# First four MLP slabs by seven products, MLP weight sums by accumulating transfers, rotary work offered to GpSimd: a two-layer fp32 encoder on one core

## The chip, the core and the metric

The kernel runs on 1 core of one Trainium2 chip. TensorE (PE) multiplies; VectorE (DVE), ScalarE (ACT) and GpSimd (POOL) work on elements; SyncE (SP) issues the loads and stores. The metric is the device time of one execution in microseconds. Three runs of the kernel before gave 1735.47, 1737.61 and 1735.81 us, a median of 1735.81.

## The reference

Two requests (256 and 512 tokens, each with 16 meta tokens put ahead: 272 + 528 = 800) go through an encoder trunk of two layers, width 1024, with shared weights:

```
for i in range(2):
    mix = mla_mixer(h, ...) if i == 0 else gqa_mixer(h, ...)
    h = layer_norm(ALPHA * h + mix)
    h = layer_norm(ALPHA * h + (relu(h @ w1) ** 2) @ w2)
return h[:, 16:]
```

The mixer of layer 0 is latent attention (dense, 16 heads, a rotary part of 32 rows for each head and one rotary key for all); the mixer of layer 1 is windowed attention with grouped heads. w1 is 1024 x 4096, w2 4096 x 1024. All is fp32 and is compared in fp32 precision.

## The kernel before

**Arithmetic.** A product in fp32 is made of three matmuls (`mm3`, L545, its matmuls L546, L547, L548): each operand is split into a high part (fp32r, a cast on ACT) and a low part (the rest, a subtraction on DVE), and high x high, high x low and low x high are summed in PSUM. Splits of weights are at L1538 (ACT) and L1544 (DVE), of hidden values at L1581 and L1583.

**Seven products for eight.** Where two output slabs and two halves of the tokens form a 2 x 2 block, the kernel uses the Strassen-Winograd scheme: seven products of blocks instead of eight, for some sums of operands before and of results after. In the input projection this is `pair` (L760 to L803), in the MLP `up_pair` for x @ w1 and `down_group` for the second product. Sums of weight blocks are made on chip by `weight_add` (L1549, the instruction L1555): a tensor_tensor on DVE or POOL over 512 columns. Sums of hidden values are `minus` (L1587, the instruction L1589); results are added to the residual by `accumulate` (L1849, L1851).

**The MLP.** It has 32 slabs of 128 hidden rows. The first four (`UP_FIRST`) are made one by one with plain products (`up_slab`), first on the first half of the tokens, while the layer norm of the attention is still being finished, then on the second. `down_first` (L1912) multiplies these four slabs with their rows of w2 in the conventional way: in layer 0 4 tiles x 2 halves x 2 outputs x 4 steps x 3 = 192 matmuls of 400 columns, in layer 1, where tokens stand on the output's partitions, 2 x 6 x 2 x 2 x 3 = 144 matmuls of 512 columns. In layer 1 the residual is turned by PE transposes (L1724) that lie between these matmuls (`TURNS`). Then six groups follow (`GROUPS`), each of two `up_pair`s (four slabs) and a `down_group` over both; the last four slabs end the layer. Weight tiles come by SP loads (L1513) of 512 KB into four raw buffers (`wraw`, with one more, `wx`), go through sums and splits, and stand in four split buffers (`wsp`) and one of half size (`w22`).

**What sets the order.** In the input projection the order on an engine is that of the code. From the attention on, tasks are handed to `Plan`, a list scheduler with costs for each engine; it can give a task to either of two engines where the code offers both (`either`, `other=`), and the order of PE's tasks comes from tables of numbers (`ORDERS`), one for each plan. Each engine runs its queue in order.

**Attention of layer 0.** For each head pair the rotary rows of the queries are made on DVE (multiply by the cosine, shuffle, multiply by the sine L1028, add, split) and copied into the heads' operand tiles (`qcopy`, L1036, 64 casts on 32 partitions). The probabilities are scaled on POOL (L1207). The rotary key's projection (`key_rope`, L604) is eight steps over the input rows, into one PSUM tile `pkr`, each step issued when its part of the input has come.

Of the kernel before, what the change touches and what calls it, by code (L numbers as in the profile page):

```python
# [20 lines left out]
P = 128  # L21
# [62 lines left out]
UPN = len(UP_FIRST)  # L84
LAST = 28
GROUPS = [(j, j + 2) for j in range(UPN, LAST, 4)]

TURNS = {1: (0, 0), 2: (0, 1), 3: (1, 0), 5: (1, 1)}  # L90
DOWN_ORDERS = ((7, 1, 6, 5, 3, 4, 2), (1, 7, 6, 5, 3, 2, 4))
# [55 lines left out]
class Plan:  # L147
# [4 lines left out]
    LAG = {"PE": 198, "DVE": 45, "ACT": 45, "POOL": 50, "SP": 0}  # L152
# [4 lines left out]
    OVER = {"PE": 0, "DVE": 82, "ACT": 100, "POOL": 30, "SP": 0}  # L157
# [56 lines left out]
    def lag(self, i, k):  # L214
        a, b = self.tasks[i][0], self.tasks[k][0]
        if a == "PE" or a == "SP":
            return 0 if a == b or a == "SP" else 198
        return {"PE": 90, "POOL": 78}.get(b, 34)

    def hold(self, i, e, cost):  # L220
        if self.thin[i]:
            return cost + 20
        return cost / 2 if e == "SP" else max(cost - self.OVER[e], cost / 2)

# [238 lines left out]
def tile_encoder(ctx: ExitStack, tc: tile.TileContext, ins: dict, y):  # L463
# [81 lines left out]
    def mm3(out, lh, ll, rh, rl, start, stop, **kw):  # L545
        nc.tensor.matmul(out, lh, rh, start=start, stop=False, **kw)  # L546
        nc.tensor.matmul(out, lh, rl, start=False, stop=False, **kw)  # L547
        nc.tensor.matmul(out, ll, rh, start=False, stop=stop, **kw)  # L548
# [16 lines left out]
    def sq_tile(pool, nm):  # L565
        return pool.tile([P, HALF], F32, tag="sq", name=f"sq{nm}", bufs=6)
# [28 lines left out]
    with ExitStack() as st:  # L595
# [6 lines left out]
        def key_rope(k, xr, c):  # L602
            for i in range(c.start // KR, c.stop // KR):
                nc.tensor.matmul(  # L604
                    pkr[32 * i : 32 * i + 32], wkr[:, k], xr[:, i * KR : (i + 1) * KR],
                    start=k == 0, stop=k == 7, tile_position=(0, 32 * i), skip_group_check=True,
                )

        for k in range(8):
# [5 lines left out]
            for c in [slice(0, HALF), slice(HALF, NT)] if k < 2 else [slice(0, NT)]:  # L615
                nc.sync.dma_start(xr[:, c], ins["xT0"][k][:, c])
                key_rope(k, xr, c)
                split(x[0][:, k, c], x[1][:, k, c], xr[:, c])
            if k % 2 == 0:
                for i in (1, 2):  # L620
                    slices[i][k // 2](nc.sync if k else None)
# [140 lines left out]
        def pair(o, u, w22, steps):  # L762
# [12 lines left out]
            def product(ps, w, c0, ops, start, stop):  # L775
                for k in range(4):
# [697 lines left out]
    def mlp_middle(mp, sqp, late_sum, T, n, l, tiles, yt=None, txs=None, ends=None):  # L1474
# [437 lines left out]
        def down_first():  # L1912
# [25 lines left out]
            for r in range(2):  # L1938
# [3 lines left out]
                for i, t in [(i, t) for t in range(6) for i in range(2)] if r == 0 else [(i, t) for a in (0, 3) for i in range(2) for t in range(a, a + 3)]:  # L1942
                    if r == i == 0 and t in TURNS:
                        turn(*TURNS[t])
                        for f in behind:
                            f()
# [790 lines left out]
```

## Time and profile before

| | |
|---|---|
| time, median of three runs | 1735.81 us |
| the profiled execution | 1735.74 us |
| its span | 1733.9 us |
| input projection | 0 to 82.5 us |
| attention of layer 0 | 82.5 to 452 us |
| MLP of layer 0 | 452 to 923 us |
| attention of layer 1 | 923 to 1234 us |
| MLP of layer 1 (last matmul) | 1234 to 1725 us |
| DVE busy, of its 2999 instructions | 1443.8 us |
| POOL busy | 220.7 us |
| bytes moved by the DMA engines | 122.32 MB |

How to read it: a time is in microseconds from the start of the span unless marked ns. A row of a timeline gives start, duration, engine, line, operation, out<-in and shape, and, in brackets, how long the engine had stood idle and what released it. A group of instructions has a count, busy time and the mean of one, then the idle time just before. A row of waits gives the total, how often and the longest. Matmuls are pipelined, so that one begins before the last has ended: the distance of two starts, and not the duration of a record, is what a matmul costs. Numbers at the end of tile names are left out in the trace; in the order rows below they are kept.

### The profile page before, as it was taken

The numbers are of one execution on the slowest core, as the hardware profiler recorded it, in microseconds if no ns is written. First come the engines' busy times: TensorE is split into PE (matmuls) and PEld (weight loads), VectorE is DVE, ScalarE is ACT, GpSimd is POOL, SyncE is SP. The second block draws the span as 40 slices with busy tenths as digits, with TensorE's granted clock in tenths as the row PEclk, the third lists the DMA queues.
The fourth block names the chain that finished last, engine by engine and source line by source line (L and its number), as shares of the span: only waits on it lengthen the run. The fifth ranks groups of instructions, "written<-read, shape, count | busy, mean of one in ns | idle before, by whom it ended". The sixth has DMA issues, their size and how long they took to land.

```text
span 1733.9 us, 28692 instructions
## 1 busy us (share of the span) xinstructions
PE 1720.2 (99%) x10826; PEld 1616.7 (93%) x10826; DVE 1443.8 (83%) x2999; ACT 1025.7 (59%) x2176; POOL 220.7 (13%) x228
## 2 busy tenths in 40 slices
PE   9999999999999999999999999999999999999998
PEld 8999999999999999999999998889989889988996
DVE  7698888986978889889886978875887899889977
ACT  6577777783745446445644728775665446545652
POOL 1211111112200000000002333232300000011000
PEclk9999999999999999999999999999999999999999
DMA  6111011104311212122123312111311221222122
GB/s 231 59 32 41 11 46 31 35 30 155 109 50 61 74 64 71 64 83 74 53 69 104 101 61 79 41 50 50 122 49 62 73 73 62 74 73 74 64 90 79
DMA packets 39019, 122.32 MB, mean 71 GB/s; under 512 B 4704, under 2 KB 9952, under 8 KB 38752
## 3 DMA queue, kind: packets, MB, share of 16 engines
q1 hardware_dynamic: 38448, 120.09, 20.8%
q8 instruction: 85, 1.39, 0.3%
q14 instruction: 54, 0.44, 0.1%
q10 hardware_dynamic: 432, 0.39, 0.1%
HBM read 117.32 MB, written 3.15 MB: 69 GB/s over the span
## 4 chain that ended last, share of the span: by engine, by line
PE 95%; DVE 3%; ACT 1%; issue 0%; DMA 0%; SPq 0%; DVEq 0%; ACTq 0%
PE w L547 18%; PE w L546 18%; PE w L548 18%; PE wb L546 4%; PE wb L547 4%; PE wb L548 4%; PE wa L546 3%; PE wa L547 3%; PE wa L548 3%; PE wa L1271 2%; PE wa L1238 2%; PE sa L546 2%; PE wb L2439 2%; PE sa L547 2%; PE sa L548 2%; PE wb L2421 2%
## 5 line engine op out<-in xcount | busy, mean ns | idle before, releaser
L1851 DVE TENSOR_TENSOR acc<-acc,w 128x400 f32<-128x400 f32 (+1 forms) x306 | 185.2, 620 | 35.2 <-PE w L548 33.4
L546 PE MATMUL w<-h,wsp 128*128 128x400 f32 x324 | 111.8, 345 | 0.0
L547 PE MATMUL w<-h,wsp 128*128 128x400 f32 x324 | 111.7, 345 | 0.0
L548 PE MATMUL w<-h,wsp 128*128 128x400 f32 x324 | 111.4, 344 | 0.0
L547 PE MATMUL w<-h,wspi 128*128 128x400 f32 x308 | 106.2, 345 | 0.0
L548 PE MATMUL w<-h,wspi 128*128 128x400 f32 x308 | 106.0, 344 | 0.0
L546 PE MATMUL w<-h,wspi 128*128 128x400 f32 x308 | 105.9, 344 | 0.0
L1583 DVE TENSOR_TENSOR h<-sq,h 128x384 fp32r<-128x384 f32 (+1 forms) x164 | 93.4, 579 | 8.8 <-ACT h L1581 8.0
L1581 ACT CAST h<-sq 128x384 fp32r<-128x384 f32 (+1 forms) x164 | 83.7, 519 | 21.7 <-DVE sq L1589 12.5
L1180 ACT ACTIVATE p<-sa,nm,rq 106x528 f32<-106x528 f32 (+1 forms) x80 | 63.5, 794 | 26.4 <-DVE nm L1177 21.4
L1207 POOL TENSOR_TENSOR p<-p,rs 106x512 f32<-106x512 f32 (+1 forms) x40 | 43.7, 1094 | 252.3 <-DVE pk L1198 139.3
L546 PE MATMUL w<-wsp,h 128*128 128x512 f32 (+1 forms) x176 | 69.3, 394 | 0.0
L548 PE MATMUL w<-wspi,h 128*128 128x512 f32 (+1 forms) x176 | 69.1, 393 | 0.0
L546 PE MATMUL w<-wspi,h 128*128 128x512 f32 (+1 forms) x176 | 69.1, 393 | 0.0
L547 PE MATMUL w<-wspi,h 128*128 128x512 f32 (+1 forms) x176 | 69.1, 393 | 0.0
L548 PE MATMUL w<-wsp,h 128*128 128x512 f32 (+1 forms) x176 | 69.1, 393 | 0.0
L547 PE MATMUL w<-wsp,h 128*128 128x512 f32 (+1 forms) x176 | 69.1, 393 | 0.0
L546 PE MATMUL sa<-k,q 128*106 128x264 f32 (+5 forms) x208 | 63.2, 304 | 1.1 <-ACT p L1190 0.7
L1762 ACT COPY sq<-w 128x400 f32<-128x400 f32 (+1 forms) x70 | 34.0, 486 | 48.5 <-PE w L548 47.9
L546 PEld LDWEIGHTS w<-h,wsp 128*128 128x128 f32 x324 | 60.9, 188 | 0.4 <-ACT sq L1762 0.2
L547 PEld LDWEIGHTS w<-h,wsp 128*128 128x128 f32 x324 | 60.8, 188 | 0.2
L548 PEld LDWEIGHTS w<-h,wsp 128*128 128x128 f32 x324 | 60.9, 188 | 0.0
(827 smaller groups left out, 6048.4 us busy)
## 6 DMA issues: line engine op xcount, KB each, us to landing
wrawo<-in_w_o_dram SPq DMA_DIRECT2D x32, 512.0 KB, 3.3
wraw0d<-in_w2b_dram SPq DMA_DIRECT2D x24, 512.0 KB, 3.3
wraw1d<-in_w2b_dram SPq DMA_DIRECT2D x18, 512.0 KB, 3.2
wrawq<-in_w_q_dram SPq DMA_DIRECT2D x8, 512.0 KB, 3.3
xr<-in_xT_dram SPq DMA_DIRECT2D x16, 200.0 KB, 3.3
wraw<-in_w_qn_dram SPq DMA_DIRECT2D x8, 384.0 KB, 3.1
wx1d<-in_w2b_dram SPq DMA_DIRECT2D x6, 512.0 KB, 4.2
out_dram<-fo SPq DMA_DIRECT2D x11, 256.0 KB, 2.0
```

What stands on the lines that cost most here:

```text
L546: nc.tensor.matmul(out, lh, rh, start=start, stop=False, **kw)
L547: nc.tensor.matmul(out, lh, rl, start=False, stop=False, **kw)
L548: nc.tensor.matmul(out, ll, rh, start=False, stop=stop, **kw)
L1180: lambda: S.activation(P_().rearrange("p (a b) -> p a b", b=264), v(), AF.Exp, bias=nm.t[:qm, 0:1], scale=sc, accum_out=rs.t[:qm, 0:1]),
L1207: f = lambda row=row, r=r, w=w: G.tensor_tensor(row()[:, META:T], row()[:, META:T], r().to_broadcast([qm, w]), ALU.mult)
L1238: nc.tensor.transpose(ps.t[:, k * qm : (k + 1) * qm], src[k], ident[:qm, :qm])
L1271: nc.tensor.matmul(av[64 * e : 64 * e + 64, :n], vt.t[:, k, h0 + 64 * e : h0 + 64 * e + 64], PT.t[:, e, k, :n], start=k == 0, stop=False, ...
L1581: plan.task("ACT", 530, lambda: S.copy(d.t[:, 0], c.t[:, :n]), reads=[c], writes=[(d, "hi")], new=[d])
L1583: "DVE", 570, lambda: V.tensor_tensor(d.t[:, 1], c.t[:, :n], d.t.bitcast(F32)[:, 0], ALU.subtract),
L1851: f = lambda: V.tensor_tensor(z, z, ps.t[:, : z.shape[-1]], ALU.add)
L2421: nc.tensor.transpose(ps.t[:, n * P : (n + 1) * P], SM.t[:, a : a + P], ident)
L2439: nc.tensor.matmul(av[64 * gi : 64 * gi + 64, :256], at["V"][:, kbs[k][0], gc : gc + 64], PT.t[:, a : a + 256], start=k == 0, stop=False, ...
```

## The change

1. `down_first` is gone. The first four slabs keep their results on the first half of the tokens (`kept`; the pool of such tiles has 8 buffers for 6), and their operands for the seven products are made like those of any group. `down_group(0, first, None)` multiplies them; w2's rows for them come as a group more (`FIRST_PAIRS`), and layer 1's transposes are all issued ahead of it.
2. Sums of weight blocks are made by transfers: `sum_in` issues, on POOL's queue, a transfer from the weights in HBM that adds to what stands in the raw tile. Each of the 28 up pairs has 4 of these of 256 KB, each of the 14 groups' down products 4 of 512 KB: 168. The blocks that a sum needs are read from HBM again. A transfer can only add, so signs are rearranged: the splits of some operands take the negative (a factor of -1 on ACT, a scalar_tensor_tensor on DVE), a relu gets the scale -1, and half of the results are subtracted.
3. In the attention of layer 0, some rotary work may go to POOL: the multiplication by the sine, the sum, the low parts of y and of the attention's result, the copies of `qcopy` and the low copies of the rotary key. 57 of the 64 casts of `qcopy` do.
4. In the input projection, the steps k = 2 to 7 of the rotary key are issued in pairs, and in `pair` the second half of the last Z product (6 matmuls) is put after the X product.
5. Two of the products' orders and the four PE tables are new.

```diff
+        def sum_in(out, src):
+            r, c = out
+            key = parts(r, c)
+            plan.task("SUM", 4500, lambda: nc.gpsimd.dma_start(r.t[:, c], src, accum_op=ALU.add), reads=key, writes=key)
...
             w22 = new("w22", lambda: mp.tile([P, 2, 512], F32R, tag="w22", name=f"w22{l}_{j}", bufs=1))
+            sum_in((b, lo), w1[j + 1][:, hi])
             split_weights(ua, lo, a, lo)
-            weight_add((a, lo), (a, lo), (b, lo), ALU.subtract, 512)
-            weight_add((b, lo), (b, lo), (b, hi), ALU.add, 512)
             split_weights(ua, hi, b, lo)
-            weight_add((b, lo), (b, hi), (a, lo), ALU.subtract, 512)
+            sum_in((b, lo), w1[j][:, lo])
+            sum_in((a, lo), w1[j + 1][:, lo])
             split_weights(ub, lo, b, lo)
-            weight_add((b, lo), (a, hi), (b, lo), ALU.subtract, 512)
+            sum_in((b, lo), w1[j][:, hi])
             split_weights(ub, hi, b, lo)
...
             out = {x: weights(f"{l}d{g}_{x}") for x in DOWN_ORDERS[l]}
-            weight_add((A21, c), (A11, c), (A21, c), ALU.subtract, w)
...
+            sum_in((A21, c), src[2, :, :w])
+            split_weights(out[1], c, A11, c)
+            sum_in((A11, c), src[1, :, :w])
+            split_weights(out[7], c, A11, c)
+            split_weights(out[5], c, A21, c)
+            sum_in((A21, c), src[0, :, :w])
+            A22 = get(2)
             split_weights(out[6], c, A21, c)
+            sum_in((A21, c), src[3, :, :w])
...
-            F[j, 0] = split_hidden(up_slab(j, 0, ws[j], twos, fill.get(j)))
+            up_slab(j, 0, ws[j], twos, fill.get(j), kept[j])
+            if j in (1, 2):
+                operands_be(first[j // 2], kept[j & 2], kept[j | 1])
...
-            F[j, 1] = split_hidden(up_slab(j, 1, w, [range(k, k + 1) for k in range(8)] if j == 0 else [range(8)]))
-        down_first()
-        for g, js in enumerate(GROUPS):
+            d = up_slab(j, 1, w, [range(k, k + 1) for k in range(8)] if j == 0 else [range(8)])
+            if j % 2 == 0:
+                operands_a(first[j // 2], kept[j], kept[j + 1], d)
+            else:
+                operands_r(first[j // 2], kept[j - 1], d)
+        if turn:
+            for hf, q in TURNS:
+                turn(hf, q)
+        down_group(0, first, None)
+        for g, js in enumerate(GROUPS, 1):
             down_group(g, [{} for _ in js], js)
...
-            plan.task("DVE", DVE(n), lambda: V.tensor_tensor(sh.t[:, :n], sh.t[:, :n], sinq[:, a:b], ALU.mult), reads=[sh], writes=[sh], port=True)
+            plan.task("DVE", DVE(n), lambda: turned(V), reads=[sh], writes=[sh], port=True, other=("POOL", POOL(n), lambda: turned(G)))
...
-            product(X, u[2], 0, TS[2], False, False)
+            x_ends = product(X, u[2], 0, TS[2], False, False)
...
-            product(Z, u[2], 512, B[1][1::2], True, True)
+            z_ends = product(Z, u[2], 512, B[1][1::2], True, True)
+            after(z_ends[2][0], x_ends[3][1])
...
-DOWN_ORDERS = ((7, 1, 6, 5, 3, 4, 2), (1, 7, 6, 5, 3, 2, 4))
+DOWN_ORDERS = ((1, 7, 6, 5, 3, 4, 2), (1, 7, 6, 5, 3, 2, 4))
...
-    "0 2-6 11 1 12 7-8 10 13-14 9 20 15 17 16 18-19 21 23 22 24 26-30 32-33 31 35 34 37 36 39 38 40 25 41-43 45 44 47-48 46 50 49 51-52"
+    "0 3 2 4-5 8 6 9 7 1 12-13 11 10 16 14 17 15 20 19 18 23 21-22 29 24 26-28 30 32 31 25 33 35 37-40 36 34 41 46 42 45 44 47-49 51 "
```

Where it moves instructions. On PE, in the input projection's `pair`, before (`inx`, `iny`, `inz` are the banks X, Y, Z; `w22i` is the last product's weight):

```order
361 L548 MATMUL iny_740<-x_134,wspi_687 128x400
362 L548 MATMUL inz_741<-x_134,wspi_724 128x400
363 L546 MATMUL inx_739<-some,wspi_724 128x400
...
373 L547 MATMUL inx_739<-tk_249,wspi_724 128x400
374 L548 MATMUL inx_739<-w22i,wspi_724 128x400
375 L546 MATMUL inx_739<-x_134,w22i 128x400
```

and after:

```order
367 L550 MATMUL inx_739<-tk_249,wspi_724 128x400
368 L551 MATMUL inx_739<-w22i,wspi_724 128x400
369 L549 MATMUL inz_741<-x_134,wspi_724 128x400
370 L550 MATMUL inz_741<-x_135,wspi_724 128x400
371 L551 MATMUL inz_741<-x_134,wspi_724 128x400
372 L549 MATMUL inz_741<-x_134,wspi_724 128x400
373 L550 MATMUL inz_741<-x_135,wspi_724 128x400
374 L551 MATMUL inz_741<-x_134,wspi_724 128x400
375 L549 MATMUL inx_739<-x_134,w22i 128x400
```

Before, the Z product was over when X's began, and X's last product follows X directly; now six matmuls of Z stand between.

On POOL, at the start of the MLP of layer 0, before (`tsum` and `sq` are sums of activations, `wraw` raw weight tiles):

```order
88 L1683 TENSOR_TENSOR tsum_5635<-acc 128x400
89 L1683 TENSOR_TENSOR tsum_5635<-acc,tsum_5635 128x400 x2
90 L1589 TENSOR_TENSOR sq_4_5697<-sq_4_5697,sq_3_5682 128x400
91 L1555 TENSOR_TENSOR wraw0d_6773<-wraw0d_6952,wraw0d_6773 128x512
92 L1589 TENSOR_TENSOR sqsum_5193<-sqsum_5193,sq_1_5671 128x400
```

and after:

```order
168 L1577 DMA wraw0d_5708<-in_w2b_dram 128x1024
169 L1708 TENSOR_TENSOR tsum_5635<-acc 128x400
170 L1577 DMA wraw0d_5684<-in_w2b_dram 128x1024
171 L1577 DMA wraw0d_5708<-in_w2b_dram 128x1024 x2
172 L1614 TENSOR_TENSOR sq_5_5700<-sq_3_5682,sq_5_5700 128x400
173 L1614 TENSOR_TENSOR sq_2_5673<-sq_3_5682,sq_2_5673 128x400
174 L1577 DMA wraw_4b<-in_w_0_dram 128x512
175 L1614 TENSOR_TENSOR sq_0_5657<-sq_4_5697,sq_0_5657 128x400
176 L1577 DMA wraw_4a<-in_w_0_dram 128x512
177 L1577 DMA wraw_4b<-in_w_0_dram 128x512
```

POOL's queue now holds the transfers of the weight sums in line with its sums of activations.

On PE, the rotary key's steps after (before, each stood alone between other matmuls):

```order
44 L550 MATMUL in_487<-x_135,wsp_65 128x400
45 L608 MATMUL pkr<-xr_180,wkr 32x200 x4
46 L608 MATMUL pkr<-xr_167,wkr 32x200 x4
47 L550 MATMUL in_255<-x_135,wsp_61 128x400
```

Two steps follow each other, and of the six visits for k = 2 to 7 three are left.

More of the change, by code (lines that the diff above doesn't have):

```diff
@@ L147 @@
 class Plan:
-    LAG = {"PE": 198, "DVE": 45, "ACT": 45, "POOL": 50, "SP": 0}
+    LAG = {"PE": 198, "DVE": 45, "ACT": 45, "POOL": 50, "SP": 0, "SUM": 0}
     CHANGE = {
@@ L156 @@
     }
-    OVER = {"PE": 0, "DVE": 82, "ACT": 100, "POOL": 30, "SP": 0}
+    OVER = {"PE": 0, "DVE": 82, "ACT": 100, "POOL": 30, "SP": 0, "SUM": 0}
     last, count = {}, 0
@@ L215, in lag @@
         a, b = self.tasks[i][0], self.tasks[k][0]
-        if a == "PE" or a == "SP":
-            return 0 if a == b or a == "SP" else 198
-        return {"PE": 90, "POOL": 78}.get(b, 34)
+        if a in ("PE", "SP", "SUM"):
+            return 198 if a == "PE" != b else 0
+        return {"PE": 90, "POOL": 78, "SUM": 78}.get(b, 34)
     def hold(self, i, e, cost):
@@ L222, in hold @@
             return cost + 20
-        return cost / 2 if e == "SP" else max(cost - self.OVER[e], cost / 2)
+        return cost / 2 if e == "SP" else 1300 if e == "SUM" else max(cost - self.OVER[e], cost / 2)
     def forward(self, deps, after, late):
@@ L545, in mm3 @@
     def mm3(out, lh, ll, rh, rl, start, stop, **kw):
-        nc.tensor.matmul(out, lh, rh, start=start, stop=False, **kw)
+        first = nc.tensor.matmul(out, lh, rh, start=start, stop=False, **kw)
         nc.tensor.matmul(out, lh, rl, start=False, stop=False, **kw)
-        nc.tensor.matmul(out, ll, rh, start=False, stop=stop, **kw)
+        last = nc.tensor.matmul(out, ll, rh, start=False, stop=stop, **kw)
+        return first.ins, last.ins
     def after(a, b):
@@ L854, in new, with split_to @@
             return plan.held(tag, make)
-        def split_to(out, view, name, reads, n, ends=(), thin=False):
+        def split_to(out, view, name, reads, n, ends=(), thin=False, pool=False):
             plan.task("ACT", ACT(n), lambda: S.copy(out()[0], view()), reads=reads, writes=[(name, "hi")], ends=ends, thin=thin)
+            rest = lambda on: on.tensor_tensor(out()[1], view(), out()[0].bitcast(F32), ALU.subtract)
             plan.task(
-                "DVE", DVE(n), lambda: V.tensor_tensor(out()[1], view(), out()[0].bitcast(F32), ALU.subtract),
-                reads=[*reads, (name, "hi")], writes=[(name, "lo")], port=True, ends=ends, thin=thin,
+                "DVE", DVE(n), lambda: rest(V), reads=[*reads, (name, "hi")], writes=[(name, "lo")], port=True, ends=ends, thin=thin,
+                other=("POOL", POOL(n), lambda: rest(G)) if pool else None,
             )
@@ L1034, in qcopy @@
                 for i, x in enumerate(("hi", "lo")):
+                    f = lambda on, e=e, i=i, row=row: on.tensor_copy(Q[s][e][i][ROPE[e] : ROPE[e] + 32], YW[s][i].bitcast(F32)[row : row + 32])
                     plan.task(
-                        "DVE", 165 + 0.5 * n, lambda e=e, i=i, row=row: V.tensor_copy(Q[s][e][i][ROPE[e] : ROPE[e] + 32], YW[s][i].bitcast(F32)[row : row + 32]),
-                        reads=[(("y", s, a), x) for a, _ in SEQ[s][3]], writes=[(("qr", s, e), x)], thin=True,
+                        "DVE", 165 + 0.5 * n, lambda f=f: f(V), reads=[(("y", s, a), x) for a, _ in SEQ[s][3]], writes=[(("qr", s, e), x)],
+                        thin=True, other=("POOL", 200 + 0.8 * n, lambda f=f: f(G)),
                     )
@@ L1067, in krope @@
                             to = K[s][e][x][r, a - 272 * s : b - 272 * s]
[L1068 removed]
+                            plan.task(
+                                on, cost(b - a), lambda copy=copy, view=view, to=to: copy(to, view), writes=[(("kr", s, e, i), ("hi", "lo")[x])],
+                                port=x == 1, ends=[st1], thin=True,
+                                other=("POOL", 200 + 0.8 * (b - a), lambda view=view, to=to: G.tensor_copy(to, view)) if x else None,
+                            )
         V_ = {}
@@ L1761, in copy @@
             def copy(d, ps, f=AF.Copy):
-                plan.task("ACT", 500, (lambda: S.copy(d.t[:, :n], ps.t[:, :n])) if f is AF.Copy else (lambda: S.activation(d.t[:, :n], ps.t[:, :n], f)), reads=[ps], writes=[d], new=[d])
+                plan.task(
+                    "ACT", 500, (lambda: S.copy(d.t[:, :n], ps.t[:, :n])) if f is AF.Copy else (lambda: S.activation(d.t[:, :n], ps.t[:, :n], f, scale=-1.0)),
+                    reads=[ps], writes=[d], new=[d],
+                )
             def plus(d, ps):
@@ L1883, in part @@
                     if ps[-1] == len(ops) - 1:
-                        accumulate(place(r, q, hf)[0], banks[q], place(r, q, hf)[1])
+                        accumulate(place(r, q, hf)[0], banks[q], place(r, q, hf)[1], ALU.subtract if r else ALU.add)
             def product(*args):
@@ L1969, in mlp_middle @@
         fill = {UP_FIRST[0]: {0: mean}, UP_FIRST[1]: {3: sums}, UP_FIRST[2]: {1: scale}}
-        F = {}
+        first = [{}, {}]
+        kept = {j: tmp(f"k{l}_{j}") for j in range(4)}
         for j in UP_FIRST:
```

186 lines of the change are left out of this document (75 added, 111 removed), and 77 rows, old and new, of the table ORDERS.

## The prediction

> **What bounds the kernel now.** I read the page first: the engines' shares and the chain that ended last.
>
> ```profile
> span 1733.9 us, 28692 instructions
> PE 1720.2 (99%) x10826; PEld 1616.7 (93%) x10826; DVE 1443.8 (83%) x2999; ACT 1025.7 (59%) x2176; POOL 220.7 (13%) x228
> PE 95%; DVE 3%; ACT 1%; issue 0%; DMA 0%; SPq 0%; DVEq 0%; ACTq 0%
> ```
>
> TensorE is busy for 99% of the span and makes up 95% of the chain. The profiled run took 1735.74 us: 1.84 us lie outside its 1733.9 us span. The three timed runs are 1735.47, 1735.81 and 1737.61, so the profiled run is the median but for 0.07 us, and what I take off its time I take off the median. Next come the stages, with columns of stretch, length, then PE, PE weight load, DVE, ACT, POOL, granted clock, DMA share, GB/s: attention of layer 0, half of its MLP, and half of the MLP of layer 1.
>
> ```profile
> 90.00:452.00 362.00, 359.78 (x2984) 335.92 (x2984) 310.37 (x859) 258.06 (x644) 62.83 (x53) 1.00 0.17 54
> 452.00:690.00 238.00, 237.82 (x1310) 236.97 (x1309) 202.51 (x341) 132.69 (x241) 12.77 (x11) 1.00 0.19 63
> 1234.00:1480.00 246.00, 245.11 (x1258) 220.94 (x1258) 213.64 (x343) 138.23 (x259) 12.86 (x11) 1.00 0.21 69
> ```
>
> The clock is full in all of them, and the MLP stretches leave PE idle for 0.18 of 238 and 0.89 of 246 us. DVE is the second engine (202.5 of 238 there, 85%). So time goes where matmuls go, or where one of PE's few idle places closes. Busy shares hide how dense PE is, since matmuls overlap: starts show that. In the timeline of PE, 128x400 and 128x512 matmuls:
>
> ```profile
> 499.79 0.35 PE L547 MATMUL w<-h,wspi 128*128 128x400 f32 x1
> ...
> 501.99 0.34 PE L547 MATMUL w<-h,wsp 128*128 128x400 f32 x1
> 1290.54 0.40 PE L547 MATMUL w<-wsp,h 128*128 128x512 f32 x1
> ...
> 1291.93 0.39 PE L547 MATMUL w<-wsp,h 128*128 128x512 f32 x1
> ```
>
> From 499.79 to 501.99 are 12 steps: 0.183 us each. From 1290.54 to 1291.93 are 6: 0.232 us each. These are the prices of one matmul, not the 0.35 and 0.39 that each record lasts.
>
> **The change, part by part.**
>
> *Down projection of the first four slabs.* By the conventional method it takes 192 matmuls of 400 columns in layer 0 and 144 of 512 in layer 1; by seven products of eight it takes 168 and 126. The order of the new program has 42 PE rows fewer, as this says. 24 x 0.183 + 18 x 0.232 = 4.39 + 4.18 = **8.57 us off**, straight from the bounding engine. Its new operands cost nothing on the path: each layer needs 14 splits of hidden operands where it had 8, and eight sums.
>
> ```profile
> L1583 DVE TENSOR_TENSOR h<-sq,h 128x384 fp32r<-128x384 f32 (+1 forms) x164 | 93.4, 579 | 8.8 <-ACT h L1581 8.0
> L1589 DVE TENSOR_TENSOR sq<-sq,sq 128x400 f32<-128x400 f32 (+1 forms) x52 | 31.3, 604 | 0.2
> L1555 DVE TENSOR_TENSOR wraw0d<-wraw0d,wraw0d 128x512 f32<-128x512 f32 x46 | 30.9, 686 | 1.5 <-DMA wraw0d<-in_w2b_dram 1.5
> ```
>
> 6 x 0.579 + 8 x 0.604 = 8.3 us of DVE, beside the second half of the four slabs, 4 x 24 x 0.183 = 17.6 us of PE. It fits if DVE has nothing else; at 85% busy it doesn't quite. What is late then is the first group's operands, and the cover is that the group begins with products 1 and 7, whose operands are made first. In layer 1 all transposes of the residual now stand ahead of the group, where before they lay between matmuls. I cost both at nothing, bounded by 0 and 2 x 8.3 / 2 = 8 us (half of that DVE work bare, in both layers). In return DVE loses the weight sums, 30.9 us in the row above alone.
>
> *Weight sums by transfers.* 168 accumulating transfers, issued on POOL's queue, take over from DVE. No trace of before shows one. The chain that grows is that of an up pair. Here is the first pair of a group in layer 0: the cast that waited for its raw tile, the last split of the third sum, and the matmul that uses it:
>
> ```profile
> 571.74 0.62 ACT L1538 CAST w<-wraw_8b 128x512 fp32r<-128x512 f32 x1 [1.01 <-DMA wraw_8b<-in_w_dram]
> 585.97 0.69 DVE L1544 TENSOR_TENSOR wspi<-wraw_8b,wspi 128x512 fp32r<-128x512 f32 x1 [0.69 <-ACT wspi L1538]
> 593.75 0.34 PE L546 MATMUL w<-h,wspi 128*128 128x400 f32 x1
> ACT wspi L1538 <- PE w L547: 44.3, 28, 4.5
> ```
>
> The weight is ready at 586.66 and used at 593.75: 7.1 us early; and ACT's splits wait for buffers that PE frees (44.3 us in 28 waits), so the weights run ahead. In the new order three sums and three splits follow one another: 3s + 3 x (0.62 + 0.69) must fit into 593.75 - 571.74 = 22.0 us, so s may be **6.0 us**. The nearest rows for s, from the list of transfers:
>
> ```profile
> wraw0d<-in_w2b_dram SPq DMA_DIRECT2D x24, 512.0 KB, 3.3
> wx1d<-in_w2b_dram SPq DMA_DIRECT2D x6, 512.0 KB, 4.2
> out_dram<-fo SPq DMA_DIRECT2D x11, 256.0 KB, 2.0
> ```
>
> Bounds: 2.0 (a plain transfer of these 256 KB) and 6.6 (twice a 512 KB load, since the destination has to be read as well as written). I take 4.2, the slowest load into the same place; then 22.0 - 12.6 - 3.9 = 5.5 us are left, and the part costs 0. At 6.6 each chain is late by 3 x 0.6 = 1.8 us. The Trainium skill, DMA: Bandwidth & Descriptors, "Anatomy of one DMA — SWDGE (gpsimd) path", fits a transfer issued from GpSimd with about 2.0 us plus its bytes at 436 GB/s; an estimate from that is 2.6 us for 256 KB, by which this term would be 0 as well; no run here shows it for an accumulate. The extra traffic is 112 x 256 KB + 56 x 512 KB = 58.7 MB beside 122 MB; by the DMA shares above (0.19 to 0.21) that still leaves the DMA engines two thirds idle.
>
> *Input projection.* The last product waits for DVE:
>
> ```profile
> 80.35 0.34 PE L548 MATMUL inx<-w22i,wspi 128*128 128x400 f32 x1
> 81.35 0.45 PE L546 MATMUL inx<-x,w22i 128*128 128x400 f32 x1 [0.66 <-DVE in L795]
> 14.59 0.35 PE L548 MATMUL in<-x,wsp 128*128 128x400 f32 x1
> 14.86 0.55 PE L604 MATMUL pkr<-xr,wkr 128*32 128x200 f32 x8
> 15.34 0.45 PE L547 MATMUL in<-x,wsp 128*128 128x400 f32 x1
> 15.63 0.34 PE L548 MATMUL in<-x,wsp 128*128 128x400 f32 x1
> ```
>
> 1.00 us pass where 0.18 would do: 0.82 lost. Six matmuls of the Z product, 1.10 us, now stand in this place: **0.8 off**. A visit to the rotary key's bank costs 15.63 - 14.59 = 1.04 us where three matmuls (one record is missing) take 0.55: 0.49, which is the visit's matmuls and its entry and exit. Three visits merge into their neighbours; between nothing and 0.49 each I take half: **0.7 off**.
>
> *Rotary work on POOL.* In layer 0's attention some casts, sums and splits leave DVE.
>
> ```profile
> L1036 DVE CAST q<-y x64: 281/420/1323, 95.7 to 350.3; 32x272 fp32r<-32x272 f32 x32, 32x528 fp32r<-32x528 f32 x32
> L957 POOL CAST q<-zero 32x528 fp32r<-32x528 f32 x2 | 1.3, 651 | 0.0
> L957 POOL CAST q<-zero 32x272 fp32r<-32x272 f32 x2 | 0.8, 403 | 0.1
> L1207 POOL TENSOR_TENSOR p<-p,rs 106x512 f32<-106x512 f32 x32 | 34.3, 1073 | 221.2 <-DVE pk L1198 108.1 <-DVE nm L1177 77.6 <-ACT acc L1297 15.4
> PE sa L546 <- ACT p L1190: 0.7, 2, 0.4
> PE sa L547 <- DVE k L860: 0.4, 1, 0.4
> PE sa L547 <- DVE k L1068: 0.2, 1, 0.2
> ```
>
> POOL needs 0.40 to 0.65 us for such a cast and is idle before its scaling of the probabilities for 221.2 us in all, in which 57 casts (at most 57 x 0.65 = 37 us) fit. Queued behind a cast is that scaling, and the transposes wait for it. PE's waits that a freer DVE could end are 0.7 + 0.4 + 0.2 = 1.3 us: bounds -1.3 and, if every cast put its extra 0.15 us in front of a scaling that is waited for, 57 x 0.15 = +8.6. I take **0.4 off**, near the first, because POOL's idle time is six times what comes. DVE's casts last 281 to 1323 ns, so something already holds some of them up. The Trainium skill, SBUF — State Buffer, "Who interferes with whom", says a DVE instruction with two SBUF inputs contends with a GpSimd instruction that reads SBUF; that speaks against this part, the spread of that row agrees, and by it the term would be nearer 0 (1725.7 in all).
>
> *Sum.* 1735.74 - 8.57 - 0.8 - 0.7 - 0.4 = 1725.3 us. The other edits (signs carried by the splits, a relu with a factor of -1, subtracting accumulations) keep the number of instructions on their engines.
>
> **The rivals.**
>
> *Late sums (slower).* If an accumulating transfer takes over 6.0 us, PE waits for the third sum of the first pair in each of 12 groups: 12 x 3 x (s - 6.0). At s = 6.6 that is 21.6 us and 1746.9. It gives all back, 10.5 us, at s = 6.3: the point from which it decides. For it: POOL's queue is in order, so a sum that waits for its raw tile holds up the next ones, and the tile is read as well as written. Against it: every plain transfer shown takes 2.0 to 4.2 us. Chance 0.13.
>
> *A start that gives back.* The first group's operands, or the transposes ahead of it, come late in both layers; or casts hold up the scaling in attention. By the bounds 4 to 8 us come back: 1729.3 to 1733.3. For it: DVE at 85% there; and on POOL's queue the sums of operands now stand behind accumulating transfers, so a transfer that waits 3.3 us for its raw tile holds an operand up as long. Against: the weight sums leave DVE, and the raw tiles are asked for early. Chance 0.15, a third of it within 0.2%.
>
> *More than the matmuls.* DVE's relief ends all 1.3 us of those waits and the merged visits give their whole 1.5: 1725.3 - 0.9 - 0.8 = 1723.6, and 1 us more of PE's idle time in the MLP goes with them: 1722.6. Chance 0.06.
>
> *No saving.* The matmuls leave, but in each layer half or more of the new 8.3 us of DVE lies bare at the same place, so that PE stands where it worked: 1725.3 + 8.6 = 1733.9. Chance 0.03.
>
> **How the numbers follow.** The forecast has 0.63. What this kernel's measurement can tell from no change is about 0.2%, 3.5 us: faster means under 1732.3. Faster: 0.63 + 0.06 + 0.10 = 0.79; within: 0.05 + 0.03 = 0.08; slower 0.13. The range goes from 1722.6, the rival below, to 1737, where sums of 6.3 us would put it; what is left out is most of the late sums and little else.
>
> **What would show it.** Right: PE rows 42 fewer with starts still 0.183 and 0.232 apart; no wait of PE on weight splits (wsp, wspi) in the MLP; sums landing in under 6 us; the 1.00 us step before the last product gone; the MLP of each layer 4 us shorter, attention of layer 0 nearly as long. Wrong: PE idle at the first up pair of each group, put down to DVE's or ACT's split; a gap at the start of the first group; scaling on POOL waited for.

## The result and the profile after

The changed kernel takes 1763.56 us (median of four runs from 1757.0 to 1765.3) where the kernel before takes 1735.82: ratio 1.0153, 95% interval 1.0136 to 1.0170. It is slower by 27.7 us, and 38 us above the forecast of 1725.3.

The page of the profiled execution (1764.8 us), engines and chain:

```profile
span 1763.0 us, 28996 instructions
PE 1724.1 (98%) x10784; PEld 1610.5 (91%) x10784; DVE 1332.7 (76%) x2776; ACT 1027.4 (58%) x2194; POOL 403.3 (23%) x466
PE 55%; DMA 20%; issue 10%; DVE 9%; ACT 5%; POOL 1%; POOLq 0%; SPq 0%; DVEq 0%; ACTq 0%
q0 software_dynamic: 24192, 58.73, 19.9%
wraw0d<-in_w2b_dram POOLq DMA_DIRECT2D x28, 512.0 KB, 5.3
wraw_4b<-in_w_dram POOLq DMA_DIRECT2D x6, 256.0 KB, 4.9
```

The view of the line that issues the sums (L1577) gives all 168 together:

```profile
DMA to landing us min/median/max: 3.6/5.2/8.4
```

PE has 42 instructions fewer, as foreseen, and DVE's busy time fell by 111 us. But PE made up 95% of the chain and now makes up 55%; transfers, absent before, have 20%. The new queue q0 holds the sums: its 58.73 MB take 19.9% of the DMA engines' span, as much as the 120.09 MB that SP's loads and stores move (20.0% on this page). A sum lands 3.6 to 8.4 us after its issue, 5.2 in the median; the page's rows are single tiles, with the size of one transfer.

By stage (an MLP goes from the start of its first matmul to the start of its last, and the other stages take what lies between):

| us | before | after | plain transfers (e4) | sums on the engines (e1) | front parts only (e11) |
|---|---|---|---|---|---|
| input projection | 83.5 | 83.5 | 81.2 | 81.5 | 81.2 |
| attention of layer 0 | 369.6 | 366.1 | 366.2 | 366.2 | 366.1 |
| MLP of layer 0 | 470.7 | 484.2 | 469.1 | 480.0 | 470.7 |
| attention of layer 1 | 310.9 | 309.7 | 309.7 | 309.6 | 311.0 |
| MLP of layer 1 | 491.5 | 511.8 | 489.9 | 494.6 | 491.5 |
| tail | 7.7 | 7.7 | 7.8 | 7.7 | 7.7 |

The two MLPs lost 13.5 + 20.3 = 33.8 us; the rest gained 4.7. Before, the stages begin at 83.5, 453.1, 923.8 and 1234.7 us; the first of these stands as 82.5 in the table of the kernel before. The input projection's "after" hides a gain: in that execution matmuls of 400 columns start 0.33 us apart until 10.2 us, where e11 has them 0.18 apart from 6.3 us on, and the later runs with the same input projection show 81.1 to 83.4.

What PE waited for in the MLP of layer 1 (total, times, longest):

```profile
PE w L549 <- ACT sq L1789: 7.5, 4, 3.9
PE w L549 <- DVE acc L1881: 3.4, 3, 2.0
PE w L550 <- DVE wsp L1566: 1.3, 3, 0.8
PE w L549 <- ACT wsp L1560: 1.2, 1, 1.2
PE w L550 <- DVE hc L1604: 0.9, 1, 0.9
PE w L551 <- DVE wspi L1566: 0.8, 1, 0.8
```

Most of it is not a weight that PE lacks (L1560, L1566 are the splits of weights): it is a copy or an accumulation out of PSUM on ACT or DVE, which has to free a bank (L1604 is a split of hidden values). Why these are late is seen in the chain of waits in a down group of layer 0 (start, duration, what):

```profile
602.86 6.94 DMA wraw0d<-in_w2b_dram
...
609.81 1.05 ACT wsp L1560
...
614.49 1.15 DVE wspi L1566
615.64 0.39 issue
616.03 5.58 DMA wraw0d<-in_w2b_dram
621.62 0.02 issue
621.64 1.06 ACT wspi L1560
622.70 0.02 issue
622.72 1.23 DVE wspi L1566
623.94 0.48 DVE acc L1881
...
628.34 0.45 PE w L549
```

One sum takes 6.9 us, a split on ACT and DVE follows, the next sum, issued only when the split has left the raw tile, takes 5.6 us, and so on. When the split of the second has ended at 623.94, DVE works off the accumulations that stood behind it in its queue, and PE, idle for 0.79 us, goes on at 628.34. A late sum thus costs twice: its weight, and the copies and accumulations out of PSUM that are queued behind its split.

A second price shows in the timeline of PE in layer 1, and in the granted clock (in the windows view, the figure behind the five engines):

```profile
1403.65 0.34 PE L551 MATMUL w<-t,wsp 128*128 128x384 f32 x1
1407.84 0.69 PE L549 MATMUL w<-t,wsp 128*128 128x384 f32 x1 [3.85 <-ACT sq L1789]
1408.33 0.53 PE L550 MATMUL w<-t,wsp 128*128 128x384 f32 x1
1408.65 0.53 PE L551 MATMUL w<-t,wsp 128*128 128x384 f32 x1
```

```profile
1406.30:1413.10 6.80, 5.26 (x16) 5.26 (x17) 5.93 (x11) 5.01 (x11) 0.00 (x0) 0.50 0.49 142
1413.10:1420.00 6.90, 6.90 (x39) 6.68 (x39) 3.10 (x5) 3.74 (x7) 1.76 (x2) 0.99 0.31 69
```

After a wait of 3.85 us the matmuls start 0.32 us apart, where 0.17 is usual: the clock is halved for 6.8 us. The trace has one more such window, of 3.4 us, in this execution: at most 10.2 / 2 = 5.1 us of the loss are clock (PE stood idle for the first 1.5 us of the longer one).

What answers to the other lines of before. At the end of the input projection the six matmuls of Z stand where the 1.00 us gap was:

```profile
80.23 0.34 PE L551 MATMUL inx<-w22i,wspi 128*128 128x400 f32 x1
80.41 0.34 PE L549 MATMUL inz<-x,wspi 128*128 128x400 f32 x1
...
81.33 0.35 PE L551 MATMUL inz<-x,wspi 128*128 128x400 f32 x1
81.51 0.36 PE L549 MATMUL inx<-x,w22i 128*128 128x400 f32 x1
```

And in attention, POOL's casts of `qcopy` by shape:

```profile
L1052 POOL CAST q<-y 32x528 fp32r<-32x528 f32 x26 | 19.2, 753 | 8.3 <-ACT y L872 5.9 <-PE sa L550 1.6
L1052 POOL CAST q<-y 32x272 fp32r<-32x272 f32 x31 | 14.3, 477 | 37.9 <-PE sa L551 24.1 <-PE sa L550 11.0 <-ACT y L872 2.1
```

57 casts take 33.5 us (37 foreseen), and no wait of PE on POOL is listed in this stage, which is shorter.

### The profile page after: what moved, and what is told of

It is laid out like the page before. It is cut to its first block, busy times and chain, and to the rows that moved or that the text cites. A ratio compares the mean times of both kernels' runs of the same rounds, so it can differ in the third digit from the quotient of the medians.

```text
span 1763.0 us, 28996 instructions
## 1 busy us (share of the span) xinstructions
PE 1724.1 (98%) x10784; PEld 1610.5 (91%) x10784; DVE 1332.7 (76%) x2776; ACT 1027.4 (58%) x2194; POOL 403.3 (23%) x466
## 3 DMA queue, kind: packets, MB, share of 16 engines
q1 hardware_dynamic: 38448, 120.09, 20.0%
q0 software_dynamic: 24192, 58.73, 19.9%
## 4 chain that ended last, share of the span: by engine, by line
PE 55%; DMA 20%; issue 10%; DVE 9%; ACT 5%; POOL 1%; POOLq 0%; SPq 0%; DVEq 0%; ACTq 0%
DMA wraw0d<-in_w2b_dram 5%; DMA wraw1d<-in_w2b_dram 5%; PE w L549 5%; PE w L551 5%; PE w L550 5%; PE wb L549 4%; PE wb L550 4%; PE wb L551 4%; PE wa L549 3%; PE wa L551 3%; PE wa L550 3%; PE wa L1293 2%; PE wa L1260 2%; DVE wsp L1566 2%; PE sa L549 2%
## 5 line engine op out<-in xcount | busy, mean ns | idle before, releaser
L1881 DVE TENSOR_TENSOR acc<-acc,w 128x400 f32<-128x400 f32 (+1 forms) x327 | 194.0, 618 | 27.0 <-PE w L551 23.8
L549 PE MATMUL w<-h,wspi 128*128 128x400 f32 x328 | 113.8, 347 | 2.8 <-DVE acc L1881 1.0
L551 PE MATMUL w<-h,wspi 128*128 128x400 f32 x328 | 113.2, 345 | 1.1 <-DVE wspi L1566 1.0
L550 PE MATMUL w<-h,wspi 128*128 128x400 f32 x328 | 113.3, 345 | 0.2 <-DVE h L1604 0.2
L549 PE MATMUL w<-h,wsp 128*128 128x400 f32 x296 | 102.8, 347 | 3.4 <-DVE acc L1881 1.5
L550 PE MATMUL w<-h,wsp 128*128 128x400 f32 x296 | 102.2, 345 | 0.2 <-DVE h L1604 0.2
L551 PE MATMUL w<-h,wsp 128*128 128x400 f32 x296 | 101.9, 344 | 0.1
L1604 DVE TENSOR_TENSOR h<-sq,h 128x400 fp32r<-128x400 f32 (+1 forms) x161 | 91.0, 573 | 12.1 <-ACT h L1604 11.4
L1604 ACT CAST h<-sq 128x400 fp32r<-128x400 f32 (+1 forms) x161 | 82.7, 518 | 29.5 <-DVE sq L1614 17.1
L1229 POOL TENSOR_TENSOR p<-p,rs 106x512 f32<-106x512 f32 (+1 forms) x40 | 42.0, 1050 | 129.5 <-DVE pk L1220 83.4
L1794 DVE TENSOR_TENSOR sq<-sq,w 128x384 f32<-128x384 f32 (+1 forms) x77 | 43.0, 559 | 37.6 <-PE w L551 37.0
L549 PE MATMUL w<-wspi,h 128*128 128x512 f32 (+1 forms) x170 | 67.9, 399 | 2.9 <-DVE acc L1881 2.9
L1577 POOL DMA_DIRECT2D wraw0d<-in_w2b_dram x28 | 24.5, 875 | 187.8 <-DVE wsp L1566 83.8
L551 PE MATMUL w<-wspi,h 128*128 128x512 f32 (+1 forms) x170 | 67.2, 395 | 0.0
L550 PE MATMUL w<-wspi,h 128*128 128x512 f32 (+1 forms) x170 | 67.2, 395 | 0.0
L549 PEld LDWEIGHTS w<-h,wspi 128*128 128x128 f32 x328 | 61.6, 188 | 5.7 <-DVE acc L1881 2.2
L1198 DVE TENSOR_REDUCE nm<-sa 106x1 f32<-106x528 f32 (+1 forms) x80 | 55.7, 700 | 14.7 <-PE sa L551 14.1
```

What stands on the lines that cost most here:

```text
L549: first = nc.tensor.matmul(out, lh, rh, start=start, stop=False, **kw)
L551: last = nc.tensor.matmul(out, ll, rh, start=False, stop=stop, **kw)
L1198: plan.task("DVE", DVE(528), lambda: V.tensor_reduce(nm.t[:qm, 0:1], v(), axis=AX.XY, op=ALU.max, negate=True), reads=[ps], writes=[nm], n ...
L1229: f = lambda row=row, r=r, w=w: G.tensor_tensor(row()[:, META:T], row()[:, META:T], r().to_broadcast([qm, w]), ALU.mult)
L1604: return lambda: S.copy(hi(), view()), lambda: V.tensor_tensor(lo(), view(), hi().bitcast(F32), ALU.subtract)
L1794: plan.task("DVE", 570, lambda: V.tensor_tensor(d.t[:, :n], d.t[:, :n], ps.t[:, :n], ALU.add), reads=[ps, d], writes=[d])
```

## The experiments

Two theories stood at first. **Late sums**: adding transfers are too long for the chain of sums and splits. **Other parts**: the first slabs' new group or the rotary work on POOL loses the time.

**e1, sums on the engines.**

```diff
-            sum_in((b, lo), w1[j + 1][:, hi])
+            weight_add((b, lo), (b, lo), (b, hi), ALU.add, 512)
...
-            sum_in((A21, c), src[2, :, :w])
+            weight_add((A21, c), (A21, c), (A22, c), ALU.add, w)
```

> The changed kernel with every weight sum made on DVE or POOL again (same signs, same order of TensorE, all other parts kept). Late sums: the accumulating transfers are the whole loss, so this gives what the other parts are worth, 1725 us (1723 to 1728), and the waits of TensorE on weights go. Rival, the other parts lose (first group's operands, rotary work on POOL): it stays above 1745 us.

Measured: 1741.41 us, ratio 1.0032 (1.0019 to 1.0046). Neither figure. The transfers do carry most of the loss, 22 us, but without them the kernel is 16 us above 1725 and slower than before, although it has 42 matmuls fewer. The first 70 us of its two MLPs (after the length, the busy time of PE comes first and that of DVE third):

```profile
447.69:517.69 70.00, 64.76 (x338) 60.77 (x338) 64.04 (x116) 43.74 (x82) 4.59 (x4) 0.98 0.13 43
1237.32:1307.32 70.00, 65.14 (x350) 56.66 (x350) 64.94 (x113) 48.42 (x96) 7.99 (x6) 1.00 0.16 52
```

The same 70 us, from the start of each MLP, in the kernel before:

```profile
453.05:523.05 70.00, 69.82 (x388) 68.98 (x388) 57.40 (x99) 41.62 (x80) 5.46 (x5) 1.00 0.17 59
1234.73:1304.73 70.00, 69.11 (x375) 61.96 (x375) 57.73 (x98) 44.21 (x90) 5.78 (x5) 1.00 0.18 61
```

DVE is busy for 64.0 and 64.9 us there (before: 57.4 and 57.7), and PE idles for 5.2 and 4.9 (before: 0.2 and 0.9), of 14.0 in both MLPs together. Nearly all of PE's waits listed there end with DVE: its splits of operands, its splits of weights and its accumulations. So the seven products for the first slabs did not pay while DVE kept the weight sums: both theories hold a part. PE's order here is the one made for the transfers; whether an order of its own would bring this kernel under 1735.8 was not tried.

**e2, sums by transfers alone.** `sum_in` and the signs put into the kernel before.

```diff
+            sum_in((b, lo), w1[j + 1][:, hi])
...
-            weight_add((a, lo), (a, lo), (b, lo), ALU.subtract, 512)
...
```

> The kernel before with the accumulating transfers and their signs alone. Late sums: 1735.8 plus the 38 us by which the changed kernel misses 1725, about 1770 us (1760 to 1780). Rival, the other parts lose: within 5 us of 1735.8.

Measured: 1809.23 us, ratio 1.0415 (1.0382 to 1.0447). The MLPs take 516.6 and 519.4 us (470.7 and 491.5 before). Worse than the 1760 to 1780 expected: in the PE order of the kernel before the loss is 73 us, and seven windows of halved clock, 37.5 us in all, stand in its trace.

**e3, the sums planned at 6000 ns.**

```diff
-            plan.task("SUM", 4500, ...
+            plan.task("SUM", 6000, ...
```

> The changed kernel, with a planned cost of 6000 ns for each weight sum in place of 4500, so that the scheduler puts the splits that follow a sum later in the queues of ACT and DVE; TensorE's order is the same. If much of the loss is other work of ACT and DVE that stands behind a split waiting for its sum: at most 1750 us. If the chain of four sums is simply too long for TensorE: 1758 us or more.

Measured: 1764.08 us, ratio 1.0149 (1.0129 to 1.0169). The same as the changed kernel, and over the 1758 us written for a chain that is simply too long. Other places in ACT's and DVE's queues don't help while PE's order stays.

**e4, plain transfers.**

```diff
-nc.gpsimd.dma_start(r.t[:, c], src, accum_op=ALU.add)
+nc.gpsimd.dma_start(r.t[:, c], src)
```

> The changed kernel with the sums' transfers overwriting the raw tile instead of adding to it (the sums of weights are left out; queue, bytes and waits are the same). If the adding makes them slow: they land in about 3 us and the time falls to 1740 us or less. If it is the queue and the bytes: landing stays at 4 to 5 us and the time above 1755 us.

Measured: 1726.39 us, ratio 0.9944 (0.9929 to 0.9959). The page, then the landing of all 168 from the view of their line:

```profile
PE 93%; DVE 5%; ACT 1%; DMA 1%; issue 0%; SPq 0%; DVEq 0%; ACTq 0%
q0 software_dynamic: 17024, 58.73, 10.3%
wraw0d<-in_w2b_dram POOLq DMA_DIRECT2D x28, 512.0 KB, 3.5
```

```profile
DMA to landing us min/median/max: 2.9/3.6/5.8
```

Same program, same queue, same bytes; only the adding is gone (and the sums with it), and with it 37 us. The same 58.73 MB take 10.3% of the DMA engines' time where the adding ones take 19.9%, and land after 3.6 us where those take 5.2. In the packets of both traces, 4096 bytes take 197 ns plain and 377 ns adding. An issue also holds POOL for less time, 0.54 us in the median against 0.87; the next runs, with adding transfers, keep the 0.87 and the number of packets. Together they show late sums to be the cause of what separates the change from 1726 us: the queue, the issue on POOL and the bytes from HBM cost it next to nothing.

**e5, e9, e12: a quarter, half, three quarters of the columns.** Each transfer adds only that part of its columns; the edit is that of e9.

```diff
-nc.gpsimd.dma_start(r.t[:, c], src, accum_op=ALU.add)
+nc.gpsimd.dma_start(r.t[:, c.start : c.start + (c.stop - c.start) // 2], src[:, : (c.stop - c.start) // 2], accum_op=ALU.add)
```

> The changed kernel with each accumulating transfer adding only the first quarter of its columns (64 or 128 KB; the rest of the sums is left out). Late sums, decided by how long one takes: it lands in about 3.6 us like the plain transfer, and the time is that of the plain transfer, 1726 us (to 1732). If adding blocks something beyond its own length (bytes in the tile, a queue that stops): above 1745 us.

> The changed kernel with each accumulating transfer adding only the first half of its columns (128 or 256 KB; the rest of the sums is left out), so that it lands at about 4.0 us, near the 4.2 us that the prediction took for a whole one. If the prediction's break-even of 6.0 us is right: 1726 to 1729 us. If the weights run late from a length between the plain transfer's 3.6 us and the whole sum's 5.2 us: 1732 to 1750 us.

> The changed kernel with each accumulating transfer adding only three quarters of its columns (192 or 384 KB; the rest of the sums is left out). Landing between the half's 3.8 us and the whole's 5.2 us, at about 4.5. If the weights have a slack that runs out at one length: a time near 1730 (not yet out) or halfway up, 1740 to 1750 us (out for the down groups' longer sums). If the loss comes from something that only whole sums do: still under 1730 us.

| adding | landing, min / median / max | time, us | ratio to before | both MLPs, us |
|---|---|---|---|---|
| a quarter (e5) | 2.6 / 3.1 / 5.7 | 1728.33 | 0.9953 (0.9938 to 0.9968) | 959.4 |
| half (e9) | 3.1 / 3.8 / 6.3 | 1727.89 | 0.9951 (0.9936 to 0.9966) | 959.5 |
| three quarters (e12) | 3.3 / 4.7 / 8.6 | 1733.66 | 0.9987 (0.9978 to 0.9996) | 968.4 |
| all (the change) | 3.6 / 5.2 / 8.4 | 1763.56 | 1.0153 (1.0136 to 1.0170) | 996.0 |

With plain transfers (e4) both MLPs take 959.0 us. The time doesn't rise with the length: it is flat up to 3.8 us, up by 6 us at 4.7 and by 36 at 5.2. That is a slack running out, and it does so between 3.8 and 4.7 us, not at 6.0. What is left between e4 and e5 or e9 lies mostly outside the MLPs: their attention of layer 0 takes 367.7 us (e4: 366.2), with one window of halved clock at 86 us. For e12 the first branch of its expectation came nearest (1734 for 1730); for e9 and e5 the low ones. That e9's low branch had been written for a break-even of 6.0 us says nothing for that figure: its transfers landed at 3.8 us, and e12 shows that the slack ends soon after. Adding by itself, with few bytes, blocks nothing.

**e6, e7: one kind of sum by transfers.** Down groups' sums on the engines (e6), up pairs' sums on the engines (e7), with `weight_add` as in e1.

> The changed kernel with the down groups' sums on DVE or POOL, the up pairs' by transfers. If the chain of four 512 KB sums of the down groups is what comes late: 1735 us (1728 to 1742). If it is the up pairs' chain: above 1750 us.

> The changed kernel with the up pairs' sums on DVE or POOL, the down groups' by transfers. If the down groups' chain comes late: above 1750 us. If it is the up pairs' chain: 1735 us (1728 to 1742).

Measured: e6 1750.92 us, ratio 1.0083 (1.0068 to 1.0098); e7 1741.27, ratio 1.0029 (1.0017 to 1.0040). Both fall on the branch written for the up pairs' chain (above 1750; up to 1742), each by less than 1 us. With up pairs by transfers the time is 9.5 us above e1, with down groups by transfers it is that of e1. But together they cost 22 more than e1: neither chain alone makes the loss, and the test did not part them as it was meant to, since each engine sum put back also loads DVE.

**e8, transfers for the first group only.** `sum_in` for the first slabs' down group and the up pair j = 4 of each layer, `weight_add` elsewhere.

> Weight sums by transfers only for the first slabs' down group and the first up pair of each layer, where DVE also makes the first group's operands; all later sums on DVE or POOL. If the 16 us that the kernel with all sums on the engines stands above 1725 are DVE's overload at the start of each MLP: 1732 us or less, faster than before. If they come from the whole MLP: 1738 us or more.

Measured: 1737.59 us, ratio 1.0013 (1.0002 to 1.0024). 3.8 us less than e1, so about a quarter of its 16 us goes with these sums. The expected 1732 was missed, and 1738, the sign of a loss in the whole MLP, just not reached. In the first 70 us of the MLPs PE still idles for 2.3 and 5.3 us (e1: 5.2 and 4.9): the gain is all in layer 0, and the start of layer 1's MLP keeps its loss though DVE no longer makes these sums; why, the run does not show.

**e10, e13: two of four sums by transfers**, adding (e10) and plain (e13).

```diff
-            sum_in((b, lo), w1[j + 1][:, hi])
+            weight_add((b, lo), (b, lo), (b, hi), ALU.add, 512)
...
-            sum_in((b, lo), w1[j][:, hi])
+            weight_add((b, lo), (b, lo), (a, hi), ALU.add, 512)
...
-            sum_in((A21, c), src[0, :, :w])
+            weight_add((A21, c), (A11, c), (A22, c), ALU.add, w)
...
```

> Two of the four sums of each chain by transfers (the second and third of an up pair; the first and second of a down group, which do not wait for each other), the other two on DVE or POOL. Late sums: each chain holds one long transfer less or two, and DVE gets half the sums back; neither limit is reached: 1726 to 1732 us, faster than both kernels. If DVE's load is the limit as soon as any sum comes back: above 1737 us.

> The kernel with two of four sums by transfers (1755 us), with these transfers overwriting instead of adding (sums of weights left out; queues, bytes and waits the same). If its loss is the length of the two transfers that are left: at most 1735 us. If it is DVE and POOL, whose sums stand in the same queues as the work of the MLP: 1745 us or more.

Measured: e10 1755.49 us, ratio 1.0110 (1.0096 to 1.0124); e13 1737.60, ratio 1.0009 (0.9999 to 1.0019). The theory of chain length missed e10 by 23 us (its range ended at 1732); the branch of DVE's load, above 1737, held. e13 fell between its two figures, 1735 and 1745. The plain form lands after 3.6 us (e10: 5.3) and takes away 18 us; the other 11 us above e4 stay, with no long transfer left, and go with the sums put back on DVE and POOL. So half as many long transfers took away 8 of the change's 37 us: each that is left is as long as before, and the engines' own sums cost time again.

**e11, front parts only.** The kernel before with the rotary work offered to POOL and that attention's new order, the paired key steps and the moved half of Z.

```diff
+            z_ends = product(Z, u[2], 512, B[1][1::2], True, True)
+            after(z_ends[2][0], x_ends[3][1])
...
+                        thin=True, other=("POOL", 200 + 0.8 * n, lambda f=f: f(G)),
```

> The kernel before with the rotary work offered to POOL (with that attention's new order), the paired steps of the rotary key and the moved half of the Z product; the MLPs are those of before. From the stages of the runs so far (2.2 us in the input projection, 3.5 us in the attention of layer 0): 1730 us (1729 to 1731.5). By the prediction's own terms, 1.9 us in all: 1733.9 us.

Measured: 1731.60 us, ratio 0.9974 (0.9964 to 0.9984). Its stages take 81.2 and 366.1 us and the rest is as before: 5.7 us less in the profiled executions, 4.1 in the medians. It is the one complete kernel here that beats both.

## Why the prediction was wrong

**The step that failed** is the sums' term: "the part costs 0", from a length of 4.2 us against a break-even of 6.0. It was worth 37 us (1763.56 against 1726.39 with plain transfers), and both figures were off. A sum takes 5.2 us in the median, outside what "the slowest load into the same place" suggests: the DMA engines need 377 ns for a packet that they need 197 for when they don't add. The upper bound's factor of two was nearly that of the packets and should have been the estimate; whether its reason, the reading of the destination, is the cause, no run shows. The length was inside the bounds, 2.0 to 6.6. And the break-even lies between 3.8 and 4.7 us (e9, e12): it was worked out on one chain, the first up pair's, with nothing in its way but its own sums and splits. The trace after shows what that left out: the down group's chain of four larger sums (5.3 us each); a sum that waits until both splits have left the raw tile; a split whose sum has landed standing in ACT's queue behind one whose sum has not (ACT stands idle for 5.18 us until the split at 708.87 us has its sum; the split behind it, at 709.39, has had its own since 706.8); and DVE's accumulations behind the split. How the loss divides among these was not parted. The rule "7.1 us early" was read from one weight and taken for all.

The traffic was under-priced too. The "two thirds idle" came from plain bytes; in the MLPs after, the DMA engines are busy for 0.54 to 0.56 of the time, and for 0.40 with plain transfers. SP's loads of 512 KB of w2 land after 4.2 to 4.3 us, where before they took 3.2 to 3.3 (e4: 3.4 to 3.7). So a raw tile comes later as well as its sums, and no run parts the two.

**The rival "late sums"** named the mechanism, and the sign, and had 0.13. By its own condition, sums of over 6.0 us, it would have cost nothing at 5.2; and its price, 21.6 us at 6.6, was too low, since a late sum also holds up copies and accumulations, and windows of halved clock follow. Its argument that the tile is read as well as written should have weighed more than loads that don't do that.

**The 42 matmuls** are gone and starts stand at 0.183 us again, but 8.57 us do not come out. With plain transfers the MLPs are 1.6 us shorter each, 3.2 together. The attention of layer 1, to which the change brings only a new PE order, gains 1.2. The rival "a start that gives back" has the traces for it. The first 70 us of the two MLPs in e4, in the windows view:

```profile
447.41:517.41 70.00, 68.43 (x376) 66.51 (x376) 65.40 (x118) 45.67 (x86) 10.71 (x13) 1.00 0.30 96
1226.17:1296.17 70.00, 67.44 (x361) 58.98 (x361) 64.99 (x106) 48.18 (x97) 13.40 (x14) 1.00 0.27 91
```

DVE is busy for 65.4 and 65.0 us (57.4 and 57.7 before), about the 8.3 us of each layer more, and PE idles for 1.6 and 2.6 (0.2 and 0.9 before). "I cost both at nothing" was wrong by these 3.1 us, of its bound of 8, and with DVE's sums back (e1) by 9.0. Another 2.3 us that the MLPs fall short of 8.57 are not placed.

**The input projection** was right: the gap has gone, the three visits are merged. 0.8 + 0.7 was foreseen, 2.3 us are there (83.5 to 81.2); which of the two gave more was not tried.

**The rotary work** was under-priced: 0.4 taken, bounds of -1.3 to +8.6, and the stage is 3.5 us shorter. Waits that end are not where this came from, as the stage before and in e11 shows (length, then PE's busy time):

```profile
83.63:453.05 369.42, 367.17 (x3043) 343.23 (x3043) 315.43 (x870) 263.38 (x661) 67.85 (x63) 1.00 0.17 55
81.41:447.37 365.96, 363.83 (x3044) 342.63 (x3043) 293.38 (x790) 261.19 (x661) 116.68 (x145) 1.00 0.17 55
```

PE idles for 2.3 us before and 2.1 in e11. What fell is its busy time, by 3.3 us for the same matmuls, so they start closer together. That would fit the new order of that attention better than the relief of DVE, but the two were not tried apart. The spread of the casts' row was read as a sign of contention between DVE instructions with two inputs and GpSimd; these casts have one input, so the row says nothing on that.

So the sum of 10.5 us came near what e4 measures (9.4 in the medians, 10.1 in the profiled executions) by luck, with terms that were wrong both ways: 3.2 + 1.2 for 8.57, 2.3 for 1.5, 3.5 for 0.4.

**The length of a transfer.** By the Trainium skill, DMA: Bandwidth & Descriptors, "Anatomy of one DMA — SWDGE (gpsimd) path", a transfer of 512 KB from GpSimd is estimated at 3.2 us; e4's plain ones land after 3.5 to 3.6, near it, and the adding ones after 5.3. For 256 KB the estimate is 2.6 us, and the rows of e4's plain ones stand at 3.0 to 4.9, those of the adding ones at 3.9 to 7.8: the fit is near for the longer plain transfers and short for the others.

## What to carry to other kernels

Price an operation that no trace shows from what it must do, here read, add and write, and not from the nearest row of another kind; then measure that one row alone before the rest. A slack is the least over all chains that use the resource, with what stands behind each waiting instruction on its in-order engine, and a time that is flat in a duration up to a point and then steep, as in the quarter, half and three-quarter runs, is its sign. Where one part of a change may pay only because another frees an engine, undo them singly and together: here the first slabs' seven products gave nothing with the weight sums back on the engines, and the small parts at the front win by themselves.

## What the runs showed of the hardware

An accumulating transfer takes about twice the DMA engines' time of a plain one: 19.9% against 10.3% of the span for the same 58.73 MB, 377 against 197 ns for a packet of 4096 bytes. Its issue holds POOL for 0.87 us in the median, that of a plain one for 0.54.

Windows of halved PE clock, 3.4 us long or twice that, follow waits of PE that are short against the span: one of 3.85 us in the change, and in e1 three of 0.48, 1.11 and 0.39 us that fell close together:

```profile
494.42 0.42 PE L549 MATMUL w<-h,wsp 128*128 128x400 f32 x1 [0.48 <-DVE acc L1885]
495.95 0.45 PE L550 MATMUL w<-h,wsp 128*128 128x400 f32 x1 [1.11 <-DVE h L1610]
...
497.53 0.45 PE L549 MATMUL w<-h,wsp 128*128 128x400 f32 x1 [0.39 <-DVE acc L1885]
...
498.74 0.54 PE L550 MATMUL w<-h,wsp 128*128 128x400 f32 x1
499.08 0.54 PE L551 MATMUL w<-h,wsp 128*128 128x400 f32 x1
```

The steps of 0.33 us last until 501.3. Not every such wait is followed by one: after a wait of 1.96 us in e8 (1294 us) there is none, and e5, e7 and e9 have one at 86 us, after a wait of 0.6 us that e4 has too, without it. What decides is not shown. The Trainium skill, TensorE: Matmul & The Clock Gate, "Part 1", says that the clock is halved after an idle window of about 3.4 us; the length of the window agrees, but in e1 PE was idle for only 2.0 of the 3.6 us before. The kernel before has no such window until after its last matmul.
